# A hybrid mLSTM and dilated-attention trunk: the third head's weighing is issued amid the fifth head's query and key products instead of amid the gate products, and the query and key slots are taken with the first result

## The chip, the cores and the metric

The kernel runs on 1 core of one Trainium2 chip, in one launch. The metric is the device time of an execution in microseconds (us). All engines belong to this one core: TensorE (PE), VectorE (DVE), ScalarE (ACT), GpSimd (POOL), and SyncE (SP), whose queue issues every transfer of this part of the program.

## What is computed

The reference runs two layers over a (1, 1024, 1024) float32 stream: an mLSTM layer (A), and a layer of dilated sliding-window attention (B) whose keys and values are projected once from the output of layer A. Only layer B matters here:

```
def dilated_attention_layer(x, w_in, w_out, kv_blocks, slopes):
    proj = x @ w_in
    q_all = proj[..., :3 * 1024].reshape(bsz, s, 3, 8, 128)
    z = proj[..., 3 * 1024:]
    outs, lses = [], []
    for g, (window, dilation) in enumerate(((128, 1), (512, 4), (2048, 16))):
        ...
        o, lse = dilated_block_attention(qb, kb, vb, dilation, window // dilation, slopes)
        ...
    wts = jax.nn.softmax(jnp.stack(lses), axis=0)
    o = jnp.sum(wts[..., None] * jnp.stack(outs), axis=0).reshape(bsz, s, 1024)
    y = o.astype(x.dtype) * jax.nn.silu(z)
    return y @ w_out
```

For each of 8 heads, three attentions (groups g = 0, 1, 2) are merged by weights that depend on the query, and the merged output is multiplied with a SiLU gate of the stream.

## The kernel before, in words

Every large product is made with three float32r matmuls (`mm3`, lines 97 to 100: high by high, low by high, high by low). An operand is split for that into a high part by ACT (a CAST, line 93) and a low part by DVE (a subtraction, line 94). The weight products use Strassen's scheme (`strassen_steps`, lines 203 to 293): seven products of 12 matmuls of 128x512 each, into PSUM banks 0 to 3; a helper on ACT (L240) or DVE (L227, L233) gathers the products, and DVE forms the sums of weight quarters that the products need (L246, L250, L263, L264) in the slots s38 and s39, where the next weights are loaded. The split weights go round through the three slots s40, s41 and s42. A tile name such as s44 is a place in SBUF, b0 to b7 are the PSUM banks.

Layer B (from line 1080) goes through two quads of heads (heads 0 to 3, then 4 to 7) and in each quad through the groups g = 0, 1, 2. For one head and one group, `queries_keys` (L1196) makes the query and key products and writes them split into the slots s44 to s47 (`qk_slots`; ACT and DVE lines 1216 and 1217), `scores` makes the scores, their maxima (L1268) and exponentials (L1272), and `attend` transposes them (L1286) and applies them to the values. After the last group of a head, `factors` (L1353) sends the head's maxima and denominators to DRAM (`ds`, L1361) and fetches them as rows (L1365 to L1369); `merge` (L1371 to L1404) makes the three weights on 8 partitions and stores them (`df`, L1404).

The **weighing** of a head then needs its three outputs, the three weights spread to all partitions, and the gate: `fetch` (L1406) loads them (gate L1412, outputs L1414, weights L1416), and `combine` (L1418) makes six 128x1024 operations on DVE: three products (L1425), two sums (L1427), and the product with the gate (L1429). `weigh` then stores the head's result `dy` (L1462). The places are fixed: the third head (head 2, counted from 0) has its running sum in s44, its second output in s46, the third in s13, the weights in s49, s51 and s52, and the gate in s50. So its running sum lies in one of the slots of the queries and keys. Which head is weighed is set by `weigh_late` (L1494): each call weighs the head whose load is under way, and starts on the next. It is called in the middle of a Strassen product, before the fifth of its steps is run (`n == 3`).

`gates` (L1468) makes the gate products of two heads, with a tanh on ACT (L1474), a DVE operation (L1475) and a store (L1477). The gates for heads 4 and 5 are made between the two quads: after group 2 of head 3 and ahead of group 0 of head 4, the fifth head. `by_group` (L1433) weighs the fourth head in three steps amid the next quad, in s50 to s52.

The program is written in one order, and a scheduler of the framework puts the instructions of each engine into a sequence by its own estimate of their times; `issue_after` and the free places bound it. On the chip each engine runs its sequence, and semaphores hold an instruction until what it needs is there.

The lines that matter: main loop 1513 to 1551, the gate call 1516 to 1520.

Of the kernel before, what the change touches and what calls it, by code (L numbers as in the profile page):

```python
# [10 lines left out]
F32 = mybir.dt.float32  # L11
F32R = mybir.dt.float32r
# [6 lines left out]
P = 128  # L19
# [18 lines left out]
def f(ap):  # L38
    return ap.bitcast(F32)
# [22 lines left out]
class Kernel:  # L62
# [1022 lines left out]
    def layer_b(self):  # L1085
# [5 lines left out]
        vs, vhl, qk_slots, sps, pts = [32, 33, 34, 35], (36, 37), (44, 45, 46, 47), (48, 49), Ring(14, 15)  # L1091
# [13 lines left out]
        def local(dst, src, g, half):  # L1105

            if g == 0:
                return dst[:, 512 * half:512 * half + 512], src
            r = 4 if g == 1 else 8
            return (dst.rearrange("p (r h i) -> p r h i", r=r, h=2)[:, :, half],  # L1110
                    src.rearrange("p (i r) -> p r i", r=r))
# [84 lines left out]

        def queries_keys(h, g, amid):

            th, tl = [[self.slot(qk_slots[2 * i + part], dtype=(F32R if g < 2 else F32))
                       if part or g < 2 else None for i in range(2)] for part in range(2)]  # L1200
            whole = self.slot(52, (P, 2, 4, P)) if g == 1 else None

            def done(half, i, aps):
                scale = (SCALE_B, 1.0)[i]
                if g == 2:
                    o, sv = local(tl[i], aps[0], g, half)
                    A.activation(o, sv, AF.Copy, scale=scale)
                    return
                dh, sv = local(th[i], aps[0], g, half)
                dl, _ = local(tl[i], aps[0], g, half)  # L1210
                if g == 1 and half == 0:

                    A.activation(whole[:, i], sv, AF.Copy, scale=scale)
                    if i == 0:
                        return
                A.activation(dh, sv, AF.Copy, scale=scale)  # L1216
                V.scalar_tensor_tensor(dl, sv, scale, f(dh), op0=ALU.mult, op1=ALU.subtract)  # L1217

            self.w_raw = raw2
            for n, _ in enumerate(self.strassen_steps(self.quarters(a["w_qk"][g, h]), x, ones, None, done, V)):  # L1220
                if n == 3:
                    amid(h)
            return [(whole, th[i], tl[i]) for i in range(2)]
# [208 lines left out]
        def by_group(h, acc, o, fb):  # L1432

            tiles = {}

            def load(g):
                tiles[g] = self.slot(o if g else acc), self.slot(fb)
                nc.sync.dma_start(tiles[g][0], self.dram["og", h, g])
                nc.sync.dma_start(tiles[g][1], self.dram["f", h][g:g + 1, :].to_broadcast([P, SEQ]))

            def step(g):
                t, acc = tiles[g][0], tiles[0][0]
                V.tensor_tensor(t, t, tiles[g][1], op=ALU.mult)
                if g:
                    V.tensor_tensor(acc, acc, t, op=ALU.add)
                if g < 2:
                    load(g + 1)
                    return
                z = self.slot(fb)
                nc.sync.dma_start(z, self.dram["z2", h])  # L1450
                V.tensor_tensor(acc, acc, z, op=ALU.mult)
                nc.sync.dma_start(self.dram["y2", h], acc)

            load(0)
            return step

        def weigh(h, fetched, behind):

            with self.tc.issue_after(behind.ins):
                acc = combine(*fetched)  # L1460
            if h < 6:
                nc.sync.dma_start(self.dram["y2", h], acc)  # L1462
            return acc
# [3 lines left out]
        def gates(c2, slots, banks=ones, sz=None):  # L1467

            keep = sz is not None
            sz = sz or [self.slot(i) for i in slots]  # L1470

            def done(half, i, aps):
                o = sz[i][:, 512 * half:512 * half + 512]
                A.activation(o, aps[0], AF.Tanh, scale=0.5)  # L1474
                V.scalar_tensor_tensor(o, o, 1.0, aps[0], op0=ALU.add, op1=ALU.mult)  # L1475
                if not keep:
                    nc.sync.dma_start(self.dram["z2", 2 * c2 + i][:, 512 * half:512 * half + 512], o)  # L1477

            yield from self.strassen_steps(self.quarters(a["w_z2"][c2]), x, banks, None, done, V,
                                           second=banks is not ones)  # L1480
# [8 lines left out]
        gate_at = {(0, 1): 0, (0, 2): 1, (1, 0): 2}  # L1489
        accs, os = Ring(44, 15), Ring(46, 50)  # L1490

        def weigh_late(h):

            nonlocal late, merged, fourth  # L1494
            if not late or late[0] > h - 2:
                return None
            acc, late = weigh(*late, self.last_plus if h < 8 else self.last_max), None
            if merged == 3:

                fourth = by_group(3, 50, 51, 52)  # L1500
            elif merged is not None:
                late = fetch_late(merged)
            merged = None
            return acc
# [6 lines left out]
        for quad in range(2):  # L1511
            heads = range(4 * quad, 4 * quad + 4)
            for h in heads:
                stats[h] = self.t(cp, [P, 2, 3, 8], tag="stat", bufs=4)
            for g in range(3):
                if (quad, g) in gate_at:
                    self.w_raw = raw2
                    for n, _ in enumerate(gates(gate_at[quad, g], qk_slots[1::2])):
                        if n == 3:
                            weigh_late(h + 1)  # L1520
                v = values(g, quad)
                for h in heads:
                    qk = queries_keys(h, g, weigh_late)
                    p = scores(h, g, qk, stats[h])
                    if h == 7 and g == 2:
                        y6 = weigh_late(8)
                    if (quad, g) == (1, 0) and h < 7:
                        with self.tc.issue_after(self.last_split.ins):
                            fourth(h - 4)
                    if g == 2:  # L1530
                        if h == 7:
                            works = 44
                        fac = factors(h, stats[h])
                    kept[h] = attend(h, g, p, head_values(g, v, h % 4, h == 4))
                    if (quad, g) == (0, 1):
                        residual(4 + h)
                    if g == 2:
                        merge(h, *fac)
                        if late:
                            merged = h  # L1540
                        elif h < 7:
                            late = fetch_late(h)
# [166 lines left out]
```

## Time and profile before

| what | value |
|---|---|
| median of 3 runs (lowest, highest) | 2009.45 us (2007.83, 2010.1) |
| the profiled execution's own time | 2008.7 us |
| its span, first to last instruction | 2006.9 us |
| TensorE busy | 1964.4 us (98%) |
| VectorE busy | 1443.5 us (72%) |
| ScalarE busy | 994.9 us (50%) |
| GpSimd busy | 159.9 us (8%) |
| mean granted TensorE clock | 0.994 of full |

Times inside the profile are counted from the span's start. In the timeline a row gives start, duration, engine, line, operation, its output and inputs with shapes, and in brackets how long the engine had been idle before it and what released it. The durations of successive rows on one engine overlap a little, so the cost of an instruction in a busy stretch is read from one start to the next.

### The profile page before, as it was taken

What the parts mean: (1) busy time and instruction counts of PE and PEld (TensorE: products, weight loads), DVE (VectorE), ACT (ScalarE), POOL (GpSimd) and SP (SyncE); (2) the same over time, 40 slices, a digit from 0 to 9 for tenths busy, and PEclk for the clock granted to TensorE, in tenths of its full rate; (3) what the DMA queues carried; (4) which work ended last, traced back from release to release, by engine and by line L of the source; (5) the groups of instructions that cost most, each with busy time, mean ns of one, the idle gap of its engine ahead of it and who ended that gap; (6) DMA issues with size and microseconds to landing.
All of it is one profiled execution on the core that took longest, in us unless ns stands there. A gap on an engine that the chain in (4) does not pass through costs nothing.

```text
span 2006.9 us, 26588 instructions
## 1 busy us (share of the span) xinstructions
PE 1964.4 (98%) x9521; PEld 1630.7 (81%) x9521; DVE 1443.5 (72%) x2854; ACT 994.9 (50%) x1990; POOL 159.9 (8%) x127
## 2 busy tenths in 40 slices
PE   9999999999999999999999999999999999999997
PEld 7788888788888888878788888877888788888776
DVE  8678788676577776457866765686469887777978
ACT  5455555535745543343524642565256456666721
POOL 0110000022145343000000000000000000000000
PEclk9999999999999999999999999999999999999999
DMA  4445465456754543516121143224335532233743
GB/s 171 140 168 193 168 220 179 149 174 227 271 205 166 191 162 118 184 62 236 53 73 48 60 144 112 71 105 163 110 107 181 193 113 85 85 105 120 264 146 126
DMA packets 115900, 293.31 MB, mean 146 GB/s; under 512 B 13428, under 2 KB 31284, under 8 KB 115768
## 3 DMA queue, kind: packets, MB, share of 16 engines
q1 hardware_dynamic: 115768, 291.61, 41.6%
q8 instruction: 75, 1.23, 0.2%
q14 instruction: 57, 0.47, 0.1%
HBM read 202.65 MB, written 88.92 MB: 145 GB/s over the span
## 4 chain that ended last, share of the span: by engine, by line
PE 83%; DVE 9%; DMA 5%; ACT 2%; issue 1%; SPq 0%; DVEq 0%; ACTq 0%
PE b L98 26%; PE b L99 25%; PE b L100 25%; DVE s L94 3%; PE b L608 1%; PE b L1286 1%; DMA s<-df 1%; DMA ds<-s 1%; PE b L614 1%; PE b L884 1%; DMA s<-in_w_v 1%; PE b L1259 1%; DVE s L233 1%; PE b L1309 1%; ACT s L93 1%
## 5 line engine op out<-in xcount | busy, mean ns | idle before, releaser
L99 PE MATMUL b<-s,s 128*128 128x512 f32 (+3 forms) x2720 | 1037.3, 383 | 6.1 <-DVE s L94 6.0
L100 PE MATMUL b<-s,s 128*128 128x512 f32 (+3 forms) x2720 | 1023.2, 382 | 3.7 <-DVE s L94 3.7
L98 PE MATMUL b<-s,s 128*128 128x512 f32 (+2 forms) x2720 | 1003.4, 387 | 12.4 <-ACT s L93 9.8
L94 DVE TENSOR_TENSOR s<-s,s 128x512 fp32r<-128x512 f32 (+2 forms) x704 | 506.5, 735 | 290.4 <-ACT s L93 286.4
L93 ACT CAST s<-s 128x512 fp32r<-128x512 f32 (+2 forms) x708 | 437.3, 636 | 560.0 <-PE b L100 322.4
L98 PEld LDWEIGHTS b<-s,s 128*128 128x128 f32 x2720 | 513.0, 189 | 115.3 <-ACT s L93 16.3
L99 PEld LDWEIGHTS b<-s,s 128*128 128x128 f32 x2720 | 513.8, 189 | 104.4 <-DVE s L94 9.4
L100 PEld LDWEIGHTS b<-s,s 128*128 128x128 f32 x2720 | 511.2, 188 | 103.3 <-DVE s L94 6.9
L233 DVE TENSOR_TENSOR s<-s,b 128x512 f32<-128x512 f32 x132 | 89.8, 681 | 31.6 <-PE b L100 30.0
L1272 ACT ACTIVATE s<-s,nmax 128x128 f32<-128x128 f32 (+1 forms) x192 | 84.4, 441 | 39.4 <-DVE nmax L1270 38.8
L94 DVE TENSOR_TENSOR s<-b,s 128x512 fp32r<-128x512 f32 (+1 forms) x96 | 51.5, 551 | 32.5 <-ACT s L93 29.6
L573 DVE SCALAR_TENSOR_TENSOR s<-s,c_convw,s 128x512 f32<-128x512 f32 (+3 forms) x96 | 71.3, 754 | 3.1 <-ACT s L570 2.6
L227 DVE TENSOR_TENSOR s<-s,b 128x512 f32<-128x512 f32 x88 | 59.5, 679 | 16.4 <-PE b L100 13.0
L318 DVE TENSOR_TENSOR s<-s,b 128x512 f32<-128x512 f32 x100 | 63.1, 679 | 9.5 <-PE b L100 5.6
L818 ACT ACTIVATE s<-s,k 128x128 f32<-128x128 f32 x144 | 47.1, 392 | 40.9 <-DVE s L94 17.4
L1268 DVE CUSTOM_DVE_ANT_0 s<-b,k 128x128 f32<-128x128 f32 (+1 forms) x192 | 57.2, 344 | 7.8 <-PE b L100 6.7
L246 DVE TENSOR_TENSOR s<-s,s 128x512 f32<-128x512 f32 x44 | 30.2, 689 | 42.4 <-DMA s<-in_w_qk 16.8
L314 DVE TENSOR_TENSOR s<-s,s 128x1024 f32<-128x1024 f32 x40 | 49.4, 1248 | 13.8 <-DMA s<-in_w_v 9.3
L93 ACT CAST s<-b 128x512 fp32r<-128x512 f32 (+1 forms) x96 | 44.0, 480 | 18.2 <-PE b L100 12.8
L777 POOL TENSOR_TENSOR s<-s 128x512 fp32r<-128x512 f32 x32 | 44.4, 1403 | 75.2 <-ACT s L776 62.0
L1217 DVE SCALAR_TENSOR_TENSOR s<-s,s 128x512 fp32r<-128x512 f32 x48 | 42.4, 883 | 9.9 <-ACT s L1216 9.4
L888 POOL TENSOR_TENSOR s<-s,s 128x512 f32<-128x512 f32 x32 | 42.5, 1343 | 65.0 <-DVE s L887 48.9
(182 smaller groups left out, 1490.4 us busy)
## 6 DMA issues: line engine op xcount, KB each, us to landing
s<-in_w_qk SPq DMA_DIRECT2D x48, 512.0 KB
s<-in_w_out SPq DMA_DIRECT2D x40, 512.0 KB
dp<-s SPq DMA_DIRECT2D x32, 512.0 KB
s<-dp SPq DMA_DIRECT2D x32, 512.0 KB
s<-in_w_v SPq DMA_DIRECT2D x24, 512.0 KB
s<-df SPq DMA_DIRECT2D x24, 512.0 KB
dn<-s SPq DMA_DIRECT2D x20, 512.0 KB
s<-dn SPq DMA_DIRECT2D x20, 512.0 KB
```

The source lines that it names most:

```text
L93: self.nc.scalar.copy(h, src)
L94: self.last_split = (l_eng or self.nc.vector).tensor_tensor(l, src, f(h), op=ALU.subtract)
L98: mm(ps, lh, rh, start=start, stop=False, skip_group_check=skip)
L99: mm(ps, lh, rl, start=False, stop=False, skip_group_check=skip)
L100: mm(ps, ll, rh, start=False, stop=stop, skip_group_check=skip)
L227: self.last_plus = V.tensor_tensor(o, p, q, op=add)
L233: V.tensor_tensor(o, p[lane][rows], q[lane][rows], op=add)
L314: eng.tensor_tensor(o[j], p[j], q[j], op=op)
L318: V.tensor_tensor(o, p, q, op=add)
L573: V.scalar_tensor_tensor(u[i][:, lo:o + 512], xm[i][:, lo - s:o + 512 - s], convw[:, c, 3 - s:4 - s], u[i][:, lo:o + 512], op0=ALU.mult, o ...
L1268: V.tensor_tensor_reduce(out=dst, in0=sc, in1=bias, op0=ALU.add, op1=ALU.max, scale=1.0, scalar=-3e38, accum_out=mx[:, b:b + 1])
L1272: self.last_exp = A.activation(res[b][0], res[b][0], AF.Exp, bias=nm[:, b:b + 1], accum_out=stat[:, 1, g, b:b + 1])
```

## The change

Two edits. The call of `weigh_late` inside the gate products goes away, so that the third head is weighed by the next call, which is the one in `queries_keys(4, 0)`, in the middle of the fifth head's first query and key product. And `queries_keys` no longer takes its four places (and s52 in group 1) on entry, but in `done`, when the first result is to be written; until then s44 and s46 belong to the third head's weighing. The lines of the changed kernel from 1206 on are numbered six higher (L1425 becomes L1431, L1216 becomes L1222, and so on). No instruction is added or removed.

```
         def queries_keys(h, g, amid):
 
-            th, tl = [[self.slot(qk_slots[2 * i + part], dtype=(F32R if g < 2 else F32))
-                       if part or g < 2 else None for i in range(2)] for part in range(2)]
-            whole = self.slot(52, (P, 2, 4, P)) if g == 1 else None
+            th, tl, whole = [None, None], [None, None], None
 
             def done(half, i, aps):
+                nonlocal whole
+                if half + i == 0:
+
+                    for part in range(2):
+                        for j in range(2):
+                            if part or g < 2:
+                                (th, tl)[part][j] = self.slot(qk_slots[2 * j + part], dtype=(F32R if g < 2 else F32))
+                    whole = self.slot(52, (P, 2, 4, P)) if g == 1 else None
                 scale = (SCALE_B, 1.0)[i]
...
                 if (quad, g) in gate_at:
                     self.w_raw = raw2
-                    for n, _ in enumerate(gates(gate_at[quad, g], qk_slots[1::2])):
-                        if n == 3:
-                            weigh_late(h + 1)
+                    for _ in gates(gate_at[quad, g], qk_slots[1::2]):
+                        pass
                 v = values(g, quad)
                 for h in heads:
                     qk = queries_keys(h, g, weigh_late)
```

How the sequences move is seen at three places.

**DVE at the end of the gates.** Before, the sequence of DVE from the low part of the fifth head's first weight (L94, s40) on: five of the six operations of the weighing (L1425, L1427) lie among the gates' operations (L1475, L233) and ahead of and behind the fifth head's weight sum (L246).

```order
L94 TENSOR_TENSOR s40_2235_13468<-s38_2228_13459,s40_2235_13468 128x512
L1425 TENSOR_TENSOR s44_2176_13138<-s44_2176_13138,s49_2178_13140 128x1024
L1475 SCALAR_TENSOR_TENSOR s47_2203_13299<-s47_2203_13299,s43_2210_13308 128x512
L1425 TENSOR_TENSOR s46_2177_13139<-s46_2177_13139,s51_2179_13141 128x1024
L233 TENSOR_TENSOR s43_2210_13308<-s43_2210_13308,b2_2208_13306 128x512
L1425 TENSOR_TENSOR s13_2162_13036<-s13_2162_13036,s52_2180_13142 128x1024
L1427 TENSOR_TENSOR s44_2176_13138<-s44_2176_13138,s46_2177_13139 128x1024
L1475 SCALAR_TENSOR_TENSOR s45_2202_13298<-s45_2202_13298,s43_2210_13308 128x512
L246 TENSOR_TENSOR s38_2228_13459<-s39_2229_13461,s38_2228_13459 128x512
L233 TENSOR_TENSOR s43_2210_13308<-s43_2210_13308,b3_2209_13307 128x512
L1427 TENSOR_TENSOR s44_2176_13138<-s44_2176_13138,s13_2162_13036 128x1024
L250 TENSOR_TENSOR s38_2228_13459<-s38_2228_13459 128x512
```

Now, from the same instruction on:

```order
L94 TENSOR_TENSOR s40_2229_13453<-s38_2222_13444,s40_2229_13453 128x512
L1481 SCALAR_TENSOR_TENSOR s47_2203_13299<-s47_2203_13299,s43_2210_13308 128x512
L233 TENSOR_TENSOR s43_2210_13308<-s43_2210_13308,b2_2208_13306 128x512
L1481 SCALAR_TENSOR_TENSOR s45_2202_13298<-s45_2202_13298,s43_2210_13308 128x512
L246 TENSOR_TENSOR s38_2222_13444<-s39_2223_13446,s38_2222_13444 128x512
L233 TENSOR_TENSOR s43_2210_13308<-s43_2210_13308,b3_2209_13307 128x512
L250 TENSOR_TENSOR s38_2222_13444<-s38_2222_13444 128x512
```

The weighing is gone from here, and the weight sums L246 and L250 follow the gates' operations directly.

**DVE between the fifth head's products and the sixth head's weights.** Now, from the first sum over the fifth head's products (L227, bank 1) to the second weight sum of the sixth head (L250, s38); all six operations of the weighing (L1431, L1433, L1435) stand in this stretch, and rows left out are marked:

```order
L227 TENSOR_TENSOR s12_2228_13452<-s12_2228_13452,b1_2225_13449 128x512
L1431 TENSOR_TENSOR s44_2174_13136<-s44_2174_13136,s49_2176_13138 128x1024
L1431 TENSOR_TENSOR s46_2175_13137<-s46_2175_13137,s51_2177_13139 128x1024
L1431 TENSOR_TENSOR s13_2162_13036<-s13_2162_13036,s52_2178_13140 128x1024
...
L1433 TENSOR_TENSOR s44_2174_13136<-s44_2174_13136,s46_2175_13137 128x1024
...
L1433 TENSOR_TENSOR s44_2174_13136<-s44_2174_13136,s13_2162_13036 128x1024
L1405 RECIPROCAL s36_2191_13239<-s36_2191_13239 8x128
L246 TENSOR_TENSOR s38_2267_13721<-s39_2268_13723,s38_2267_13721 128x512
L1223 SCALAR_TENSOR_TENSOR s47_2238_13531<-s12_2228_13452,s46_2236_13529 128x512
L1435 TENSOR_TENSOR s44_2174_13136<-s44_2174_13136,s50_2179_13141 128x1024
L1409 TENSOR_TENSOR s36_2191_13239<-s36_2191_13239 8x128 x3
L250 TENSOR_TENSOR s38_2267_13721<-s38_2267_13721 128x512
```

Before, this stretch held none of the six; it held two operations L1217 where one L1223 stands now, two L1396 where one L1402 stands, and two L94 (one of them the sixth head's s41) where three L94 stand.

**ACT at the same place.** Before, the fifth head's first copy (L1216, s44 from bank 0) stands ahead of all casts for the sixth head's weights (L93 from s38_2271):

```order
L1216 ACTIVATE s44_2224_13455<-b0_2230_13463 128x512
L93 CAST s41_2278_13734<-s38_2271_13725 128x512
L1216 ACTIVATE s46_2225_13456<-s12_2234_13467 128x512
L93 CAST s42_2279_13751<-s38_2271_13725 128x512
L1216 ACTIVATE s44_2224_13455<-s12_2234_13467 128x512
L93 CAST s40_2280_13767<-s38_2271_13725 128x512
L1216 ACTIVATE s46_2225_13456<-s12_2234_13467 128x512
L240 COPY s43_2277_13733<-b0_2273_13729 128x512
```

Now the copy into s44 comes after the three casts, since s44 has to be stored first:

```order
L93 CAST s41_2274_13730<-s38_2267_13721 128x512
L1222 ACTIVATE s46_2236_13529<-s12_2228_13452 128x512
L93 CAST s42_2275_13747<-s38_2267_13721 128x512
L93 CAST s40_2276_13763<-s38_2267_13721 128x512
L1222 ACTIVATE s44_2235_13528<-b0_2224_13448 128x512
L1222 ACTIVATE s44_2235_13528<-s12_2228_13452 128x512
L1222 ACTIVATE s46_2236_13529<-s12_2228_13452 128x512
L1278 ACTIVATE s48_2243_13593,stat_2198_13294<-s48_2243_13593,nmax_2245_13595 128x128
```

Bank 0 is held until that copy. PE's sequence is changed to suit: the sixth head's first products are those into banks 2 and 1 (weights s42 and s40), and the product into bank 0 (s41) comes after them; before, it came first. Within the fifth head, the product into bank 1 ends 26 matmuls after the start of the one into bank 2, where it was 36.

## Rows read from the trace of the kernel before

**Rows 1.** The page: busy time of the engines, and the shares of the chain of work that ended last, by engine.

```profile
PE 1964.4 (98%) x9521; PEld 1630.7 (81%) x9521; DVE 1443.5 (72%) x2854; ACT 994.9 (50%) x1990; POOL 159.9 (8%) x127
...
PE 83%; DVE 9%; DMA 5%; ACT 2%; issue 1%; SPq 0%; DVEq 0%; ACTq 0%
```

**Rows 2.** Stretches of 2 us at the end of the gates: length, then busy time (and number of instructions) of PE, its weight loads, DVE, ACT and POOL, the granted TensorE clock, the share of the DMA engines, GB/s.

```profile
1576.00:1578.00 2.00, 0.00 (x1) 0.01 (x1) 2.00 (x5) 0.68 (x2) 0.00 (x0) 0.98 0.96 367
1578.00:1580.00 2.00, 1.22 (x2) 0.50 (x2) 2.00 (x3) 2.00 (x4) 0.00 (x0) 0.50 0.18 61
...
1582.00:1584.00 2.00, 2.00 (x6) 1.58 (x5) 2.00 (x5) 0.00 (x0) 0.00 (x0) 0.50 0.94 308
```

**Rows 3.** Timeline of PE from the last matmul ahead of its wait to the return of its usual pace; ten matmuls are left out after 1578.00.

```profile
1574.71 0.40 PE L100 MATMUL b<-s,s 128*128 128x512 f32 x1
1578.00 0.80 PE L98 MATMUL b<-s,s 128*128 128x512 f32 x1 [2.88 <-ACT s L93]
...
1580.48 0.79 PE L98 MATMUL b<-s,s 128*128 128x512 f32 x1 [1.26 <-ACT s L93]
...
1584.48 0.52 PE L98 MATMUL b<-s,s 128*128 128x512 f32 x1
1584.84 0.40 PE L99 MATMUL b<-s,s 128*128 128x512 f32 x1
1585.07 0.39 PE L100 MATMUL b<-s,s 128*128 128x512 f32 x1
```

**Rows 4.** Timeline of DVE in the same stretch.

```profile
1566.62 0.69 DVE L94 TENSOR_TENSOR s<-s,s 128x512 fp32r<-128x512 f32 x1 [0.77 <-ACT s L93]
1570.20 1.23 DVE L1425 TENSOR_TENSOR s<-s,s 128x1024 f32<-128x1024 f32 x1 [2.90 <-DMA s<-df]
1571.34 0.69 DVE L1475 SCALAR_TENSOR_TENSOR s<-s,s 128x512 f32<-128x512 f32 x1
...
1573.68 1.22 DVE L1425 TENSOR_TENSOR s<-s,s 128x1024 f32<-128x1024 f32 x1
1574.82 1.22 DVE L1427 TENSOR_TENSOR s<-s,s 128x1024 f32<-128x1024 f32 x1
1575.95 0.68 DVE L1475 SCALAR_TENSOR_TENSOR s<-s,s 128x512 f32<-128x512 f32 x1
1576.55 0.68 DVE L246 TENSOR_TENSOR s<-s,s 128x512 f32<-128x512 f32 x1
```

**Rows 5.** Timeline of ACT in the same stretch.

```profile
1566.49 0.63 ACT L1474 ACTIVATE s<-s 128x512 f32<-128x512 f32 x1
...
1577.33 0.62 ACT L93 CAST s<-s 128x512 fp32r<-128x512 f32 x1 [2.90 <-DVE s L246]
```

**Rows 6.** Timeline of SP's queue: the spread weights of the third head, the second half of the fifth head's weights (s39), and the small loads of the fourth head's maxima.

```profile
1563.15 1.27 SPq L1416 DMA_DIRECT2D s<-df  x3
1564.52 0.38 SPq L180 DMA_DIRECT2D s<-in_w_qk  x1
...
1574.74 0.62 SPq L1368 DMA_DIRECT2D s<-ds  x2
```

**Rows 7.** Timeline of DVE from the first sum over the fifth head's products to the second weight sum of the sixth head.

```profile
1590.50 0.69 DVE L227 TENSOR_TENSOR s<-s,b 128x512 f32<-128x512 f32 x1 [0.16 <-PE b L100]
1591.10 0.38 DVE L1396 TENSOR_TENSOR s<-s 8x128 f32<-8x128 f32 x1
1591.41 0.67 DVE L94 TENSOR_TENSOR s<-s,s 128x512 fp32r<-128x512 f32 x1
...
1596.24 0.67 DVE L246 TENSOR_TENSOR s<-s,s 128x512 f32<-128x512 f32 x1
...
1598.21 0.67 DVE L250 TENSOR_TENSOR s<-s 128x512 f32<-128x512 f32 x1
```

**Rows 8.** Timeline of ACT: the cast that follows L246 there.

```profile
1597.02 0.62 ACT L93 CAST s<-s 128x512 fp32r<-128x512 f32 x1 [2.05 <-DVE s L246]
```

**Rows 9.** Waits of PE from 1600 us to the end, the largest: the line that waited, for what, us in total, times, longest.

```profile
PE b L98 <- ACT s L93: 1.9, 2, 1.8
```

**Rows 10.** Two other places where PE was idle for over 1.5 us (timeline of PE).

```profile
996.06 0.50 PE L99 MATMUL b<-s,s 128*128 128x512 f32 x1 [2.47 <-DVE s L94]
1945.12 0.50 PE L98 MATMUL b<-s,s 128*128 128x512 f32 x1 [1.76 <-ACT s L93]
```

**Rows 11.** Stretches of 2 us behind these two places (columns as in group 2).

```profile
996.00:998.00 2.00, 1.94 (x8) 1.61 (x9) 2.00 (x4) 0.35 (x2) 0.00 (x0) 1.00 0.00 0
...
1948.00:1950.00 2.00, 2.00 (x6) 1.59 (x5) 0.00 (x0) 0.00 (x0) 0.00 (x0) 0.51 0.00 0
```

**Rows 12.** Timeline of SP's queue: the store of the first head's result from s44, and the next transfer, which loads into s44.

```profile
1525.18 0.43 SPq L1462 DMA_DIRECT2D dy<-s  x1
1530.24 0.32 SPq L1414 DMA_DIRECT2D s<-dg  x1
```

**Rows 13.** The chain of waits around the gates: start, us, what; the store of the fourth head's maxima and denominators.

```profile
1565.00 9.34 DMA ds<-s
```

**Rows 14.** Two longer stretches in which the first and the second head were weighed amid queries and keys of group 2 (columns as in group 2).

```profile
1500.00:1520.00 20.00, 20.00 (x109) 16.95 (x109) 18.36 (x46) 12.07 (x29) 0.00 (x0) 1.00 0.43 150
1540.00:1560.00 20.00, 18.92 (x102) 15.92 (x101) 19.81 (x49) 12.40 (x28) 0.00 (x0) 1.00 0.49 167
```

**Rows 15.** Timeline of DVE at the end of the program: the weighing of the last head.

```profile
1937.61 2.60 DVE L1425 TENSOR_TENSOR s<-s,s 128x512 f32<-128x512 f32 x4 [5.47 <-DMA s<-df]
```

## The prediction

> **What bounds the kernel.** Read the page first: TensorE is busy 98% of the span and holds 83% of the chain that ended last [rows 1]. A microsecond is won or lost only where PE waits or runs at its lower clock. The median is 2009.45 us; the sums below are differences against the profiled execution (2008.7 us, span 2006.9 us, 1.8 us around it), which stands 0.75 us under that median, so a difference is added to 2009.45. About 0.2%, 4.0 us, is what a measurement of this kernel can tell from no change.
>
> [...] The timeline of PE gives its price: 2.88 and 1.26 us idle, then matmuls 0.43 us apart where 0.23 is usual, until 1584.84 [rows 3]. Without the stop, the twelve matmuls between 1574.71 and 1584.84 would have run from 1574.94, 0.228 us apart, to 1577.67. The place costs 1584.84 − 1577.67 = **7.2 us**: 4.1 idle, 3.0 lower clock.
>
> Then the cause. PE waited for a cast of ACT, ACT waited 2.90 us for DVE's weight sum L246 [rows 5], and DVE came to L246 only at 1576.55 because the first weighing operation L1425 stood ahead of it and waited 2.90 us for the spread weights `df` [rows 4]. L1475, whose input from ACT was there at 1567.1 [rows 5], stood behind it too. The change moves exactly these operations.
>
> **What the change removes.** The six weighing operations leave this place; L1477's stores and the small loads L1365 to L1369 follow earlier on SP's queue, and nothing on PE waits for those. But L246 adds two halves of the weights, s38 and s39, and s39 is loaded behind the three spread weights: issued at 1564.52 [rows 6]. It cannot be expected ahead of the first of these (1570.20 [rows 4]); and in the sequence with its waits, the first L1368 is held on the semaphore which that load raises, and went out at 1574.74 [rows 6]. I take 1573.7, when the third L1425 found the third spread weight there [rows 4]. From L246 to PE's matmul it took 1578.00 − 1576.55 = 1.45 us [rows 3, 4], so PE restarts at 1575.15 instead of 1574.94, and at 1576.2 at the worst bound. The third matmul needs the low part (L94), which now stands behind L246, L233 and L250: 3 × 0.60 + 0.67 = 2.5 us after L246's start, where PE gets to it after 1.45 + 0.46 = 1.9: 0.6 more. Left over are 0.6 to 1.9 us; taken 0.8. **Gain: 6.4 us** (5.3 to 6.6).
>
> **What it moves in.** The six operations now lie between the first sum over the fifth head's products (L227) and the sixth head's weight sums. Before, L227 to the start of L246 took 1596.24 − 1590.50 = 5.74 us [rows 7]. Now three L1431 and two L1433 are added, 1.14 us each (1573.68 to 1574.82 [rows 4]), 5.68; an L94 is added (0.60, as 1575.95 to 1576.55 for that shape [rows 4]), two L1217 become one (−0.60), and one L1396 goes (−0.31 [rows 7]); the one L1217 that remains moves behind L246 (−0.60). That gives 10.5 us. From L246 to L250 it was 1.97 us [rows 7]; L1435 (1.14) and L1223 (0.60) come in and L233 goes out (−0.59): 3.1. So L250 starts 13.6 us behind L227.
>
> PE has little to cover this. When the bank-1 product is done, which L227 followed at once (idle 0.16 [rows 7]), 46 matmuls are left ahead of the sixth head's first: 46 × 0.228 = 10.5 us. That first needs the cast behind L246: 0.78 us from L246 to the cast [rows 7, 8] and 0.67 from cast to matmul [rows 3, 5], so it runs 0.2 + 10.5 + 0.8 + 0.7 = 12.2 us behind the product's end: 1.7 us idle. Two matmuls (0.46) later, PE needs the cast behind L250, 3.1 us after the first: 2.7 us idle. The product into bank 0, 12 matmuls or 2.7 us, stood first before and would cover the wait; now it stands behind, because bank 0 is read late (next paragraph). **Loss: 4.4 us idle**, wherever on the time axis L227 falls, since both chains start from it. If the sixth head's s39, whose load waits for the last reader of that slot behind the three L1431, is late, some 0.5 more.
>
> The clock: 4.1 us of idle time at the gates brought 3.0 us of lower clock [rows 2, 3]; 1.76 us brought it too at 1945, 0.51 [rows 10, 11], while 2.47 us at 996 did not, 1.00 [rows 10, 11]. With two waits so close, as at the gates, I take it that the clock falls; the longer wait comes last and hides part of the slow stretch, so I take **2.2 us** (0 to 3.0).
>
> The first copy into s44 now waits for the store of the third head's result. Its price is bounded by the store of another head from s44, behind which the next transfer into s44 could be issued 5.06 us later [rows 12]. L1435 ends 13 us behind L227, say at 1595; the store is there by 1600.3, s44 and bank 0 are free by about 1602. PE comes to bank 0 at about 1604: no wait. Behind it the maxima and exponentials of the fifth head's first scores run later against PE than before; transposes that need them come 0.3 and 0.6 us too early by my count of the sequences: **about 1 us** (0 to 2).
>
> Behind that, PE waits little up to the end (the largest line 1.9 us in all [rows 9]), and only the order of SP and DVE near the end changes: 0.
>
> **Sum:** −6.4 + 4.4 + 2.2 + 1.0 = +1.2 us, so 2010.65 us; with the bounds, −6.6 + 4.4 = −2.2 up to −5.3 + 4.9 + 3.0 + 2.0 = +4.6. The forecast is **no change that can be measured, 2010.6 us**.
>
> **Rivals.**
> A, faster: the new place costs nothing, because ACT, DVE and PE keep more distance than my chains say. For it: from 1500 to 1520, a head was weighed amid queries and keys, and PE was busy 20.00 of 20.00 us [rows 14]. Against it: there, scores and attention of group 2 lie between, and already the next weighing (1540 to 1560) has 18.92 [rows 14]. It gives −6.4: **2003.0 us**.
> B, slower: the store of the result out of s44. ACT's copy L1222 waits for it, and behind that copy on ACT are all exponentials of the fifth head and the gathering of bank 0 for the sixth. What waits first on an engine holds what is ready behind it: L1475, ready at 1567.1, ran at 1571.34 behind L1425 at the gates [rows 4, 5]. A small store took 9.34 us there, amid other transfers [rows 13]. A landing later than about 1603 decides: at 1595 + 9.3 = 1604.3 PE loses about 2 us more and a second slow stretch of up to 3.0, so +1.2 + 5 = +6.2: **2015.6 us**. For it: two loads of 512 KB stand right ahead of this store on SP's queue.
> [...]
> C, the end: the last head's weighing waits 5.47 us for `df` [rows 15] and PE 1.76 us for what follows, with a slow stretch behind it [rows 10, 11]. The changed order of transfers there could take this away or double it: −4 to +5, **2005.5 or 2014.5 us**.
> D: the change does not do what it says. The sequences show it does; only a scheduler's order on paper, unlike the chip's, is left: 2009.4 us.
>
> **Chances.** Forecast 0.45, A 0.22, B 0.19, C 0.12 (0.05 faster, 0.07 slower), D 0.02. Faster by over 0.2%: A and C's 0.05, 0.27. Within: 0.45 + 0.02 = 0.47. Slower: B and C's 0.07, 0.26. The forecast's own range is 2007.3 to 2014.1. The whole range reaches A's time and nearly B's, 2003.0 to 2015.0, which leaves out about half of A and half of B, 0.2.
>
> **What would show it.** Right: near 1575 no stop of PE over 1 us and a clock of 1.00; DVE idle some 5 us ahead of L246 for a weight load; near 1592 to 1598 two stops of PE behind ACT's casts, 1.7 and 2.7 us, and a stretch at the lower clock; six weighing operations between L227 and L250. A: no stop there. B: a stop of PE near 1604, ACT idle ahead of L1222 for the store `dy`. Wrong altogether: a stop left at 1575, because s39 lands late, or a difference that arises after 1620 only.

## The result, and the profile after

| what | before | after |
|---|---|---|
| median of 6 runs (lowest, highest) | 2007.67 us (2004.17, 2010.1) | 2017.37 us (2012.53, 2021.19) |
| the profiled execution's own time | 2008.7 us | 2021.19 us |
| its span | 2006.9 us | 2019.4 us |
| mean granted TensorE clock | 0.994 | 0.992 |

The ratio of the changed kernel to the kernel before is 1.0048 (95% interval 1.0034 to 1.0061): 9.7 us slower, where 1.2 us slower, too little to measure, was forecast. The profiled execution is the slowest of its six runs; it stands 12.5 us above the profiled one of before.

On the page of the kernel after, the busy times are hardly others than before [rows 1]. In the chain that ended last, PE's share falls from 83% to 76%, and DVE, transfers and issue hold more.

```profile
PE 1969.9 (98%) x9521; PEld 1632.3 (81%) x9521; DVE 1443.8 (71%) x2854; ACT 994.1 (49%) x1990; POOL 158.9 (8%) x127
...
PE 76%; DVE 11%; DMA 7%; issue 3%; ACT 2%; SPq 0%; DVEq 0%; ACTq 0%
```

The timeline of PE in the kernel after, all stops of 0.18 us and over that the text speaks of (start, duration, operation, and in brackets the idle time ahead of it and what ended it; rows between are left out), shows the time at once:

```profile
1577.54 0.50 PE L98 MATMUL b<-s,s 128*128 128x512 f32 x1 [0.39 <-ACT s L93]
...
1578.64 0.50 PE L100 MATMUL b<-s,s 128*128 128x512 f32 x1 [0.37 <-DVE s L94]
...
1590.95 0.47 PE L98 MATMUL b<-s,s 128*128 128x512 f32 x1 [1.58 <-DVE s L227]
...
1597.20 0.50 PE L98 MATMUL b<-s,s 128*128 128x512 f32 x1 [0.18 <-ACT s L93]
...
1600.29 0.80 PE L98 MATMUL b<-s,s 128*128 128x512 f32 x1 [2.35 <-ACT s L93]
...
1614.72 0.33 PE L1292 MATMUL b<-c_ident,s 128*128 128x128 f32 x1 [0.68 <-ACT s L1278]
...
1631.75 0.47 PE L98 MATMUL b<-s,s 128*128 128x512 f32 x1 [1.35 <-DVE s L233]
...
1632.93 0.50 PE L100 MATMUL b<-s,s 128*128 128x512 f32 x1 [0.48 <-DVE s L94]
...
1957.15 0.79 PE L98 MATMUL b<-s,s 128*128 128x512 f32 x1 [4.51 <-ACT s L93]
```

The stop at the gates [rows 3] is down to 0.39 and 0.37 us. In its place stand four: near 1591 to 1600 (the fifth head's last products and the sixth head's first weights), at 1615 (transposes of the fifth head's scores), at 1632 (the seventh head's weights), and at 1957, the end, where 4.51 us stand for the 1.76 of before [rows 10].

To compare executions, PE's lost time is added up over stretches: for each matmul, the time from its start to the next one's start, less the median of that time for matmuls of its shape in the same trace. Idle time and lower clock are both in it. At the gates of before this gives 7.06 us, where the prediction had 7.2.

| stretch, us | what lies there | before | after | difference |
|---|---|---|---|---|
| 1560 to 1584 | gates, fifth head's first weights | 7.06 | 1.54 | −5.5 |
| 1584 to 1610 | fifth head's products, sixth head's weights | 0.38 | 6.70 | +6.3 |
| 1610 to 1625 | fifth head's scores | 0.04 | 1.95 | +1.9 |
| 1625 to 1645 | seventh head's weights | 0.15 | 4.09 | +3.9 |
| 1645 to 1925 | the heads behind | 7.1 | 7.7 | +0.6 |
| 1925 to 1975 | the last head's weighing | 3.62 | 6.83 | +3.2 |

These add up to 10.4 us. The other 2.1 us of the 12.5 between the two profiled executions were there by 1560, where both run the same sequence (the first exponentials of the fourth head's group 2 start at 1556.96 and at 1559.02). Such differences come and go: up to 1560 all twelve profiled executions of this document run that sequence, and they lost 43.8 to 51.0 us there.

**The place that the weighing moved to.** The timeline of DVE in the kernel after, in the same stretch as [rows 4, 7] (rows between are left out):

```profile
1576.09 0.69 DVE L246 TENSOR_TENSOR s<-s,s 128x512 f32<-128x512 f32 x1 [4.03 <-DMA s<-in_w_qk]
...
1585.25 0.67 DVE L227 TENSOR_TENSOR s<-s,b 128x512 f32<-128x512 f32 x1
1585.85 3.48 DVE L1431 TENSOR_TENSOR s<-s,s 128x1024 f32<-128x1024 f32 x3
...
1590.14 0.67 DVE L227 TENSOR_TENSOR s<-s,b 128x512 f32<-128x512 f32 x1
...
1593.81 1.21 DVE L1433 TENSOR_TENSOR s<-s,s 128x1024 f32<-128x1024 f32 x1
...
1595.81 0.62 DVE L246 TENSOR_TENSOR s<-s,s 128x512 f32<-128x512 f32 x1
...
1598.84 0.67 DVE L250 TENSOR_TENSOR s<-s 128x512 f32<-128x512 f32 x1
...
1620.15 0.68 DVE L94 TENSOR_TENSOR s<-s,s 128x512 fp32r<-128x512 f32 x1
...
1629.04 0.69 DVE L246 TENSOR_TENSOR s<-s,s 128x512 f32<-128x512 f32 x1 [2.38 <-DMA s<-in_w_qk]
```

Three things are to be seen. At the gates DVE waits 4.03 us for the weights in s39 and not for `df`. From L227 (bank 1) to L246 it takes 10.56 us and to L250 13.59, where before it took 5.74 and 7.71 [rows 7]. And in between, the second L227 (bank 2) stands behind the three L1431; PE's next product into bank 2 waits for it, 1.58 us.

**What that delays.** The timeline of SP's queue after, from the store of the third head's result to the next weights:

```profile
1598.18 0.32 SPq L1468 DMA_DIRECT2D dy<-s  x1
...
1602.74 4.94 SPq L1445 DMA_DIRECT2D s<-df  x2
1620.86 0.33 SPq L180 DMA_DIRECT2D s<-in_w_qk  x1
1621.99 0.32 SPq L1445 DMA_DIRECT2D s<-df  x1
1622.59 0.33 SPq L180 DMA_DIRECT2D s<-in_w_qk  x1
```

Before, both of these weight loads (L180, for the seventh head) were issued from 1607.46 on, as the timeline of SP's queue before shows:

```profile
1607.46 5.31 SPq L180 DMA_DIRECT2D s<-in_w_qk  x2
```

The waits of SP's queue from 1600 to 1645, in the kernel after (line that waited, for what, us in total, times, longest), name what held them, the low part that reads the slot last:

```profile
SPq L180 <- DVE s L94: 25.8, 3, 13.1
```

The kernel before has that wait too (23.7 us in total, the longest 13.9); what changed is when it ends. There the low part came at 1606.74, here at 1620.15. The second load landed 6.32 us after its issue by the chain of waits (a row of start, us, what), DVE's sum waited 2.38 us for it (above, 1629.04), and PE 1.35 and 0.48 us for what follows:

```profile
1622.59 6.32 DMA s<-in_w_qk
```

### The profile page after: what moved, and what is told of

Same layout as the page of the kernel before. It is cut to its first block, busy times and chain, and to the rows that moved or that the text cites. A ratio compares the mean times of both kernels' runs of the same rounds, so it can differ in the third digit from the quotient of the medians.

```text
span 2019.4 us, 26584 instructions
## 1 busy us (share of the span) xinstructions
PE 1969.9 (98%) x9521; PEld 1632.3 (81%) x9521; DVE 1443.8 (71%) x2854; ACT 994.1 (49%) x1990; POOL 158.9 (8%) x127
## 4 chain that ended last, share of the span: by engine, by line
PE 76%; DVE 11%; DMA 7%; issue 3%; ACT 2%; SPq 0%; DVEq 0%; ACTq 0%
PE b L98 24%; PE b L100 23%; PE b L99 23%; DVE s L94 3%; PE b L608 1%; DMA s<-in_w_qk 1%; DMA s<-df 1%; PE b L1292 1%; ACT s L93 1%; PE b L614 1%; PE b L884 1%; DMA s<-in_w_z 1%; DVE s L233 1%; DMA s<-in_xq 1%; DMA s<-in_w_v 1%
## 5 line engine op out<-in xcount | busy, mean ns | idle before, releaser
L98 PE MATMUL b<-s,s 128*128 128x512 f32 (+2 forms) x2720 | 1004.5, 387 | 21.2 <-ACT s L93 13.6
L94 DVE TENSOR_TENSOR s<-s,s 128x512 fp32r<-128x512 f32 (+2 forms) x704 | 507.5, 735 | 284.3 <-ACT s L93 279.0
L93 ACT CAST s<-s 128x512 fp32r<-128x512 f32 (+2 forms) x708 | 437.3, 636 | 554.0 <-PE b L100 304.8
L233 DVE TENSOR_TENSOR s<-s,b 128x512 f32<-128x512 f32 x132 | 89.7, 680 | 27.5 <-PE b L100 26.5
L94 DVE TENSOR_TENSOR s<-b,s 128x512 fp32r<-128x512 f32 (+1 forms) x96 | 51.2, 551 | 31.9 <-ACT s L93 31.7
L227 DVE TENSOR_TENSOR s<-s,b 128x512 f32<-128x512 f32 x88 | 59.5, 679 | 15.5 <-PE b L100 12.1
L246 DVE TENSOR_TENSOR s<-s,s 128x512 f32<-128x512 f32 x44 | 30.2, 687 | 54.6 <-DMA s<-in_w_qk 20.7
L314 DVE TENSOR_TENSOR s<-s,s 128x1024 f32<-128x1024 f32 x40 | 49.3, 1248 | 14.8 <-DMA s<-in_w_v 10.4
L93 ACT CAST s<-b 128x512 fp32r<-128x512 f32 (+1 forms) x96 | 43.7, 479 | 17.6 <-PE b L100 12.7
L1222 ACT ACTIVATE s<-s 128x512 fp32r<-128x512 f32 x48 | 42.1, 879 | 18.0 <-DVE s L233 16.6
L777 POOL TENSOR_TENSOR s<-s 128x512 fp32r<-128x512 f32 x32 | 43.8, 1384 | 76.1 <-ACT s L776 67.3
L1223 DVE SCALAR_TENSOR_TENSOR s<-s,s 128x512 fp32r<-128x512 f32 x48 | 42.2, 882 | 9.6 <-ACT s L1222 9.3
```

What stands on the lines that cost most here:

```text
L93: self.nc.scalar.copy(h, src)
L94: self.last_split = (l_eng or self.nc.vector).tensor_tensor(l, src, f(h), op=ALU.subtract)
L98: mm(ps, lh, rh, start=start, stop=False, skip_group_check=skip)
L227: self.last_plus = V.tensor_tensor(o, p, q, op=add)
L233: V.tensor_tensor(o, p[lane][rows], q[lane][rows], op=add)
L314: eng.tensor_tensor(o[j], p[j], q[j], op=op)
```

## The experiments

All ratios are to the kernel before, with a 95% interval; each group ran on one chip beside runs of the kernel before (medians 2009.9, 2010.72 and 2010.27 us). "Lost" is PE's lost time as above.

**The first group: is it the slot s44, or DVE's time?**

*The changed kernel once more.*

> The changed kernel once more, to see which of its stops come back. Theory: all four do, since they follow from the sequences: PE stops near 1590 (about 1.6 us, a bank read late by DVE), 1600 (2.3), 1615 (0.7), 1630 (1.8, weights loaded late) and at the last head's weighing (4.5 instead of 1.8); 8 to 12 us slower than before. Rival: the stop near 1630 or the one at the end belongs to that one execution; then it is missing here and the kernel is 4 to 7 us slower.

Ratio 1.0044 (1.0029 to 1.0058), median 2019.82. The stops come back at the same places: 1.59, 0.18 and 2.34 us near the sixth head's weights, 0.68 at the scores, 1.35 and 0.48 at the seventh head's weights, 4.61 at the end. Lost 6.92, 1.94, 3.02 and 6.47 us in the four stretches that hold them. These are the kernel's, not one execution's.

*The third head's running sum in s15 instead of s44.*

```diff
-        accs, os = Ring(44, 15), Ring(46, 50)
+        accs, os = Ring(44, 15, 15, 15, 44, 15), Ring(46, 50)
```

> The change, but the third head's running sum lies in s15 instead of s44, so no copy of the fifth head's queries waits for its store. The six weighing operations stay where the change put them; the sequence at the end of the program is that of the kernel before. Theory (the shared slot makes most of the cost: bank 0 is held, the sixth head's products and the seventh's weights come late): stops near 1600, 1615 and 1630 go, one stop of 1 to 2 us stays near 1590 to 1600, the end is as before: 4 us faster than before (3 to 6). Rival (the six operations on DVE make the cost wherever the sum lies): the stops of 4 us and the lower clock between 1588 and 1604 stay, so within 1 us of before. The end: 1.8 us of PE stop if its sequence sets it.

Ratio 0.9990 (0.9978 to 1.0001), median 2008.18. The six operations still stand amid the fifth head, but the store no longer holds the fifth head's s44. In the sequences, the sixth head's product into bank 0 stands first again. ACT's copy out of bank 0 into s44 shows it in the timelines, here with s15 and then in the changed kernel, where it waits for the store of the result:

```profile
1581.54 0.60 ACT L1222 ACTIVATE s<-b 128x512 fp32r<-128x512 f32 x1 [1.59 <-PE b L100]
```

```profile
1601.08 0.60 ACT L1222 ACTIVATE s<-b 128x512 fp32r<-128x512 f32 x1 [0.84 <-DMA dy<-s]
```

The timeline of DVE in this kernel shows that its own path with s15 is no shorter, 12.83 us from L227 to L246:

```profile
1580.11 0.67 DVE L227 TENSOR_TENSOR s<-s,b 128x512 f32<-128x512 f32 x1
1580.71 3.48 DVE L1431 TENSOR_TENSOR s<-s,s 128x1024 f32<-128x1024 f32 x3
...
1592.94 0.67 DVE L246 TENSOR_TENSOR s<-s,s 128x512 f32<-128x512 f32 x1
```

Yet of PE's stops, in its timeline, two are left there:

```profile
1585.81 0.47 PE L98 MATMUL b<-s,s 128*128 128x512 f32 x1 [1.59 <-ACT s L93]
...
1595.66 0.50 PE L100 MATMUL b<-s,s 128*128 128x512 f32 x1 [0.50 <-DVE s L94]
```

The first is that of bank 2, which falls ahead of 1584 here. Lost 3.85 us from 1560 to 1645, that stop included, where the changed kernel lost 14.27; behind 1610 they are 0.16 and 0.15, against 1.95 and 4.09, and the seventh head's loads go out from 1603.58. At the end 3.64 are lost, as before (3.62). So it is the slot: one change of place takes back the whole loss. PE's twelve matmuls into bank 0, some 2.7 us, stand ahead of DVE's path again and cover the stop of 2.35 us. The 4 us faster that were expected are not shown: the interval reaches from 4.4 us faster to no change.

*The third head is not weighed*: six operations are left out, and its first output is stored as it is.

```diff
-                acc = combine(*fetched)
+                acc = combine(*fetched) if h != 2 else fetched[0][0]
```

> The change without the third head's six weighing operations (left out: its output is stored unweighed). Theory and both rivals agree that the stops from 1588 to 1640 go and that the gates' stop is below 1 us: 5.8 us faster than before, less what the sequence at the end costs, which is a third one here (0 to 3 us): 3 to 6 us faster. If it is not faster than before, the gain at the gates is lost to something that none of them names.

Ratio 0.9983 (0.9973 to 0.9994), median 2007.0. Lost 1.52 us from 1560 to 1645, where the kernel with s15 lost 3.85 and after 14.27. So without the six operations there is little to gain beyond s15: the loss isn't DVE's time by itself, but needs the late result in s44.

*The weights spread behind s39.* The third head's spread weights are loaded behind the fifth head's weights, and the weighing begins at the end of the gates, behind L246 and L250.

```diff
-                if n == 3:
+                if (h, g, n) == (4, 0, 0):
+                    amid(h)
+                if n == 3 and (h, g) != (4, 0):
...
+            if late[0] == 2:
+                with self.tc.issue_after(self.last_raw.ins):
+                    spread(2, late[1][1], fbs)
```

> The third head is weighed where the kernel before weighs it, but its spread weights are loaded behind the second half of the fifth head's weights (s39), and L246 and L250 stand ahead of the six operations on DVE. Theory: PE's stop at the gates came of L246's place behind operations that waited for the spread weights, so it goes (below 1 us) and nothing comes in its place, since the six operations lie over 12 products of the fifth head from 1572 to 1585: 6 us faster than before, less up to 3 us for another sequence at the end. Rival (any place near the fifth head costs DVE time that PE needs): a stop of 2 us or more between 1580 and 1600, and no more than 2 us faster.

Ratio 1.0017 (1.0007 to 1.0027), median 2013.52. The theory was wrong here. The stop at the gates is gone, L246 is back at 1572.29, and the scores and the seventh head lose nothing (0.09 and 0.17). But the six operations, from 1574.70 to 1585.6, now stand ahead of the fifth head's own later weight sum (L264 at 1585.56), and PE stops for that:

```profile
1586.93 0.50 PE L98 MATMUL b<-s,s 128*128 128x512 f32 x1 [1.65 <-ACT s L93]
...
1589.13 0.79 PE L100 MATMUL b<-s,s 128*128 128x512 f32 x1 [1.46 <-DVE s L94]
```

With a clock of 0.50 from 1590 to 1594 that loses 6.57 us, and the end 7.66. Six operations of 1.14 us ahead of a weight sum cost about as much here as the slot did there: both matter, in different places.

**The second group: the end, and bank 2.**

*Two splits of the output weights behind the last head's shares.* In the timeline of DVE after, splits of the output weights (L94, 128x1024) run amid the last head's merge, the last two at 1935.78, ahead of its last operations; the weighing behind it then waits 5.82 us for `df`:

```profile
1935.78 2.34 DVE L94 TENSOR_TENSOR s<-s,s 128x1024 fp32r<-128x1024 f32 x2
...
1949.61 2.57 DVE L1431 TENSOR_TENSOR s<-s,s 128x512 f32<-128x512 f32 x4 [5.82 <-DMA s<-df]
```

These two splits are held until the merge's last operation.

```diff
-                V.tensor_tensor(d, t, o, op=ALU.mult)
+                self.last_share = V.tensor_tensor(d, t, o, op=ALU.mult)
...
-            with self.tc.issue_after(self.last_exp.ins):
+            with self.tc.issue_after((self.last_share if c >= 6 else self.last_exp).ins):
```

> The change, with two DVE operations moved: the low parts (L94, 128x1024) of the output weights of the last two heads stand behind the last head's merge instead of amid it; no other instruction of any engine moves. Theory (the end costs more because that merge, and so the store of df7, comes later in DVE's sequence): df7 goes out 2.3 us earlier against what stands ahead of it, PE's stop at the end falls from 4.5 to 2.2 us, lost time from 1925 on from 6 to 3.5; 2 to 3 us faster than the change, 6 to 8 us slower than the kernel before. Rival (the transfers around df7 set the end, not DVE's sequence): the stop stays at 4 us or more.

Ratio 1.0021 (1.0013 to 1.0029), median 2015.71. Nothing else moves in the sequences. In the timeline of DVE the two splits now come behind the shares (L1409), and the wait for `df` is shorter:

```profile
1938.06 0.86 DVE L1409 TENSOR_TENSOR s<-s 8x128 f32<-8x128 f32 x3
1938.85 2.34 DVE L94 TENSOR_TENSOR s<-s,s 128x1024 fp32r<-128x1024 f32 x2
...
1945.05 2.59 DVE L1431 TENSOR_TENSOR s<-s,s 128x512 f32<-128x512 f32 x4 [3.87 <-DMA s<-df]
```

PE's stop is 2.38 us at 1952.61 instead of 4.51, and the end loses 4.24 us instead of 6.83 and 6.47. The order of two operations that are not part of the change sets this. The median gained more than the end shows, some 4 us against 2.2 to 2.6. In the profiled execution the stop of 2.35 us at 1600 is there, but no lower clock behind it (1.00 from 1600 to 1604); whether that holds for the others, no trace shows.

*The weighing one step later* (behind the product into bank 2), with s44.

```diff
-                if n == 3:
+                if n == (4 if (h, g) == (4, 0) else 3):
```

> The change, but the six weighing operations come behind the second sum over the fifth head's products (L227, bank 2) and no longer ahead of it; the sum stays in s44. Theory (one chain of DVE sets both stops, and s44 holds bank 0): the stop near 1590 goes, and the stops near 1597 and 1600 grow by as much; lost time from 1584 to 1610 stays at 6 to 7.5, the one near 1630 stays: 8 to 11 us slower than before. Rival (the bank that is read late costs by itself): 1.6 to 2 us faster than the change.

Ratio 1.0048 (1.0031 to 1.0065), median 2021.14. The stop of bank 2 goes to bank 3 (1.36 us at 1588.94, for L233), and 1.37 and 2.24 us follow for the sixth head's weights. Lost 14.1 us from 1560 to 1645, as in the changed kernel (14.3). The stop of bank 2 is no cost by itself.

*The same with s15.*

> As the kernel with the sum in s15, but the six operations come behind the second sum over the fifth head's products. Theory (with s44 free, PE has bank 0's product to cover DVE, and the only stop left there is bank 2's): lost time from 1560 to 1645 falls from 3.9 to 2.5, 1.5 us faster than the sum in s15, 3 us faster than before or a little more. Rival (the six operations cost what they cost, wherever they are put): the same as with the sum in s15 within 0.5 us, with a stop of 1.5 us further on.

Ratio 1.0007 (0.9997 to 1.0017), median 2012.87. The theory failed: 6.4 us are lost from 1560 to 1645 instead of 3.85, by stops of 1.39 us (for L233), 0.74 (sixth head's weights) and 1.45 (`nmax` of the scores). With s15, too, the place of the six operations counts.

*Both, with the two splits later.*

> The sum in s15, the six operations behind bank 2's sum, and the two output-weight splits behind the last head's merge. If the parts add: 1.5 us at bank 2 and 2 to 3 us at the end on top of the kernel with the sum in s15: 5 to 7 us faster than before. If the end is set by transfers: as without the two splits moved, 3 us faster.

Ratio 0.9992 (0.9981 to 1.0003), median 2008.5. Lost 5.8 us from 1560 to 1645, 0.8 at the end. The parts do not add up to the 5 to 7 us that were expected: the place behind bank 2 costs amid the fifth head nearly what it did without the splits (6.4).

**The third group: the version that the experiments point to.**

*s15 and the two splits later.* The diffs of the second and the fifth experiment together.

> The sum in s15, six operations where the change put them, and the two output-weight splits behind the last head's merge. Theory (both parts are real and lie in different places): lost time from 1560 to 1645 near 3.9 instead of 8.1, from 1925 on near 0.5 instead of 3.0: 5 to 7 us faster than before, faster than the change by 13 to 16. Rival (what is won amid the fifth head is lost again at the end): within 2 us of before.

Ratio **0.9978** (0.9969 to 0.9987), median 2004.98: faster than the kernel before by 4.4 us by the ratio and by 5.3 between the medians, at the lower end of what was expected, and faster than the changed one. All of PE's stops of 0.3 us and over from 1570 to 1645 and from 1925 to 1975:

```profile
1590.34 0.47 PE L98 MATMUL b<-s,s 128*128 128x512 f32 x1 [1.56 <-DVE s L227]
1600.18 0.50 PE L100 MATMUL b<-s,s 128*128 128x512 f32 x1 [0.53 <-DVE s L94]
```

Lost 3.6 us from 1560 to 1645, and nothing (−0.1) at the end.

*The kernel before, with the two splits later.*

> The kernel before, with only the two output-weight splits behind the last head's merge. Theory: PE's stop at the end (1.8 us and a stretch at the lower clock, 3.0 us in all) shrinks to below 1; 2 to 3 us faster than before; the stop at the gates stays at 7 us. Rival (transfers set the end): no change.

Ratio 0.9991 (0.9981 to 1.0001), median 2009.0: not to be told from no change. The end loses next to nothing (0.2 instead of 3.6), the gates stop 1.47 and 1.75 us and lose 6.45 in all. Between this kernel and the one above, which ran on the same chip, lie 4.0 us in the medians, and 3.2 in the lost time from 1560 to 1645 (6.7 and 3.6). That is what the weighing's new place gives with its result out of the way.

## Why the prediction was wrong

**The gates: right.** 6.4 us were to go (5.3 to 6.6), 5.5 went in the first execution of after and 6.0 in the second (lost 1.05). L246 was to run when s39 lands, 1573.7 or some time later; it ran at 1576.09, which is 1574.0 on the axis of before, behind a wait of 4.03 us for that load.

**DVE's path to the sixth head's weights: right in size.** The chains of 10.5 and 13.6 us, counted instruction by instruction, came out at 10.56 and 13.59. Of the 4.4 us idle forecast, 4.11 came, but split otherwise: 1.58 for the second L227, which the prediction did not list, and with that already waited for, 0.18 and 2.35 instead of 1.7 and 2.7. The sum held because all these waits hang on one chain of DVE. With the lower clock 6.3 and 6.5 us were lost, where 4.4 + 2.2 = 6.6 were forecast; here the size of the clock term was a choice within its range. Rival A (nothing lost there) is refuted.

**What failed: the step behind the sixth head's weights.** "Behind that, PE waits little up to the end … and only the order of SP and DVE near the end changes: 0", and "about 1 us" for the scores. The zero rested on how little PE waited there before [rows 9]; what the change moves there was not worked out. Behind 1610 the kernel after lost 9.6 us more than before, nearly all of it in three places:

- The scores: "about 1 us" (0 to 2); 1.9 measured in both executions, twice the size taken and just within its bound.
- The seventh head's weights: not in the sum; +3.9 and +2.9. The prediction saw that the product into bank 0 moves behind the others, and asked only whether PE would have to wait there (it did not). It did not ask which slot comes free later for it. The first of the seventh head's loads waits for a low part (L94) of the sixth head's weights, the last reader of its place; that came at 1620.15, and the load was issued at 1620.86 instead of 1607.46. With s15, bank 0 stands first and this loss is gone (0.15).
- The end: 0 taken; +3.2 and +2.9. The store of the last head's `df` went out at 1943.82 instead of 1932.17, 11.7 us later, of which about 9 are the delay from above. The prediction had this as rival C, and had its slower side (up to +5) at 0.07. That two splits amid the merge set 2 us of PE's stop is shown by the two kernels in which only these were held back. But they are not what the changed kernel loses more than before: in the kernel before, too, they stand ahead of the merge's end and cost 3.4 us, and with them moved in both, 4.24 us against 0.22 are lost. What does differ is the seventh head. Before, its `df` goes out at 1896.01 and its weighing begins at 1905.92 (rows from the timelines of SP's queue and of DVE; the last is the store of the last head's `df`):

```profile
1896.01 0.29 SPq L1404 DMA_DIRECT2D df<-s  x1
1905.92 1.21 DVE L1425 TENSOR_TENSOR s<-s,s 128x1024 f32<-128x1024 f32 x1
1932.17 0.29 SPq L1404 DMA_DIRECT2D df<-s  x1
```

After, both come 18 to 19 us later, twice the delay, and so the weighing lies later in the last head's merge, behind a wait of 2.03 us:

```profile
1915.05 0.34 SPq L1410 DMA_DIRECT2D df<-s  x1
1923.80 1.23 DVE L1431 TENSOR_TENSOR s<-s,s 128x1024 f32<-128x1024 f32 x1 [2.03 <-DMA s<-df]
1943.82 0.29 SPq L1410 DMA_DIRECT2D df<-s  x1
```

That this makes the difference at the end was not tried by itself.

**Rival B named the right slot and the wrong wait.** The store from s44 was issued at 1598.18, and ACT's copy into s44 ran at 1601.08: 2.90 us, earlier than the 1603 from which it would have decided. ACT waited 0.84 us for it, and PE did not stop for bank 0. The prediction had bounded this by the 5.06 us of [rows 12]. What s44 costs is the sequence: with bank 0 held until s44 is stored, twelve matmuls stand behind the wait that they would have covered. That DVE's path was no shorter with s15 and yet the stop of 2.35 us gone shows it. Why the scheduler chose that order is read from the sequences, not tried; and the other place of the sum moves more of the sequences than these twelve matmuls, so what each move is worth was not separated.

Added up, −5.5 + 6.3 + 1.9 + 3.9 + 0.6 + 3.2 = +10.4 us of lost time, against 9.7 in the medians. The forecast's terms for the first two came to −6.4 + 6.6 = +0.2, measured +0.8; its error lies in the rest. The prediction named "a difference that arises after 1620 only" as a sign that it would be wrong altogether: 7.7 of the 10.4 us arose behind 1625, on top of what it had counted.

## What to carry to other kernels

When work moves, follow its result's slot as well as its time: here the slot that was stored late held the PSUM bank that was to be copied into it (the copy ran 2.90 us behind the issue of the store), then the order of the products (a stop of 2.35 us), then the slots of the next weights (the first load issued at 1620.86 instead of 1607.46), and the last of these was 30 us away. Where a scheduler sets the sequence, a shift of the order can be a cost of its own, at the far end too (here 3.2 and 2.9 us more were lost at the end): compare the sequences up to the last instruction, and give no place a zero because nothing of the change stands there. And cover counts by position: a DVE path of 10 to 13 us cost 6.7 us in the changed kernel, with twelve matmuls behind it, and 2.7 in the kernel with s15 and the two splits later, with them ahead (lost time from 1584 to 1610).

## What the runs showed of the hardware that was not expected

The lower clock did not follow here from the length of a stop alone. These are stretches of 2 us of the kernel after, behind the stops at 1591, 1600 and 1632 (columns as in [rows 2]; the clock is the third number from the end):

```profile
1592.00:1594.00 2.00, 1.95 (x9) 1.28 (x8) 2.00 (x5) 0.09 (x1) 0.00 (x0) 1.00 0.73 236
...
1600.00:1602.00 2.00, 1.71 (x4) 1.42 (x5) 2.00 (x5) 1.16 (x3) 0.00 (x0) 0.50 0.99 325
...
1634.00:1636.00 2.00, 2.00 (x6) 1.61 (x5) 1.88 (x4) 0.76 (x2) 0.00 (x0) 0.50 0.00 0
```

1.58 us brought none, 2.35 us did, and 1.35 and 0.48 us did. But in the repeated run the same stops at 1632 brought none (1.00 from 1632 to 1638), and in the changed kernel with the two splits later the same 2.35 us brought none (1.00 from 1600 to 1604). A term for the lower clock is thus a range, as the prediction had it (0 to 3.0), and one trace does not settle it. The same sequences up to 1560 us lost 43.8 to 51.0 us in PE in single executions, which is why a kernel of 2000 us is told apart by a few us only with many runs.
